# Prompt attention of a hybrid encoder step: weight blocks of which 16 queries are used, transposed from 32 rows

## The chip, the cores and the metric

The kernel runs on one core of one Trainium2 chip. The metric is the device time of one execution in microseconds; a number in a table is the median of the runs of a kernel, and one execution is also taken with the hardware profiler.

## The reference, cut to what matters

The reference computes one step of a one-layer streaming encoder: stick-breaking attention and a Mamba-2 state-space branch in parallel, a gated merge, and a causal convolutional FFN, for one new stream (16 meta tokens and 1024 frames) and for 8 running streams of 16 frames. The change lies in the attention of the new stream, 16 heads of 64 dimensions:

```python
def stick_breaking(q, k, v, q_pos, k_pos):
    z = jnp.einsum('bqhd,bshd->bhqs', q, k).astype(jnp.float32) * (SB_HEAD_DIM ** -0.5)
    reach = k_pos[None, :] < q_pos[:, None]
    log_beta = jax.nn.log_sigmoid(z)
    log_keep = jnp.where(reach, jax.nn.log_sigmoid(-z), 0.0)
    later = lax.cumsum(log_keep, axis=3, reverse=True) - log_keep
    w = jnp.where(reach, jnp.exp(log_beta + later), 0.0)
    return jnp.einsum('bhqs,bshd->bqhd', w.astype(v.dtype), v)
```

A query reaches only keys before it. So the weights `w` of a block of queries are zero from its own position on, and the transposed weights are needed only for the queries that reach a block of keys at all.

## The kernel before, in words

The program runs in phases: input norms, the state-space branch, the prompt attention (`phase_att`), the attention of the running streams (`phase_smp`), the merge, and the FFN. In `phase_att` the 16 heads follow each other (`head`, from L703), and projections of q, k, v and of the gates, which do not depend on the heads, are handed in between them (`paced`, L976) so that TensorE has other work while a head waits. The order of the instructions on each engine is not written out by hand: a scheduler of the framework works it out for the whole program from its own estimates of durations, and each engine then runs its list in that order.

A head works on its 1024 queries (the first two of 1026 are done elsewhere) in two groups g of four blocks i of 128 queries. For a block i:

- the scores of its queries against L = 144 + 128 i keys, `z` (L732, L735), on PE;
- a sigmoid on ACT (L695) into `beta`, the mask and 1 - beta on POOL (L741, L698), the running product over the keys from the end on DVE (L699), and the product that gives the weights, still in `beta` (L701).

The weights of a block lie with 128 queries on the partitions and keys along the row. The product with the values needs keys on the partitions, so each 128x128 piece is transposed by PE. `T_` (L133 to L135) does that: the piece is loaded as the stationary operand and the identity matrix streams through. For each block j of 128 keys up to 4g + 2, one PSUM tile `wT` takes the transposed pieces of the blocks i of the group side by side, 128 columns for each. There are two such buffers. The queries of block i sit at positions 16 + 128 i to 143 + 128 i, so of the queries of block i = j - 1 only the last 16 reach keys of block j. `b0` is therefore max(4g, j - 1), and `lo` skips 112 columns where the first piece is such a one; but the whole piece of 128 rows is transposed. ACT casts `wT` from `lo` on to a rounded high part `wTh` (L97), DVE takes the rest as `wTl` (L98), and two products on PE add both into `po`, tile `o` (L756, L759).

The remainder (from L760) holds the pieces (i, j) = (2, 4g + 3), (3, 4g + 3), (3, 4g + 4), where i counts within the group. They go into one `wT` tile at columns 0, 128 and 256, ACT copies columns 112 to 384 of it to `wf32` (L764), and plain float32 products of 144 and of 16 queries follow (L766). The first and the third of these pieces are used only in their last 16 queries. Then `att` is put together (L768, L769) and stored.

So in each group four transposes are of pieces of which only 16 queries are used: those at j = 4g + 1 and j = 4g + 2, and two in the remainder.

Of the kernel before, what the change touches and what calls it, by code (L numbers as in the profile page):

```python
# [13 lines left out]
F32 = mybir.dt.float32  # L14
# [63 lines left out]
class Kernel:  # L78
# [51 lines left out]
        l = self.tile(pool, [128, T], F32R, 'sl')  # L130
        return h, l

    def T_(self, out, in_, m=None):  # L133
        k = in_.shape[0]
        self.nc.tensor.transpose(out, in_, self.ident[:k, :k])  # L135


    def setup(self):
# [564 lines left out]
    def head(self, h, v):  # L703
        nc, ap, pa = self.nc, self.ap, self.pa
        marks = []
        rows = slice(64 * h, 64 * h + 64)
        KH, KL = (self.tile(ap, [128, TP], F32R, f'{n}{h % 2}', bufs=1) for n in ('KH', 'KL'))
        QS = self.tile(ap, [128, TP - T0], F32R, f'QS{h % 2}', bufs=1)
        VV = self.tile(ap, [128, 9, 128], F32R, f'VV{h % 2}', bufs=1)
        for r in (slice(0, 64), slice(64, 128)):  # L710
            nc.sync.dma_start(KH[r].bitcast(F32), self.s_kh[rows, 0:TP])
            nc.sync.dma_start(KL[r].bitcast(F32), self.s_kl[rows, 0:TP])
        nc.sync.dma_start(QS[0:64].bitcast(F32), self.s_qh[rows, 0:TP - T0])
        nc.sync.dma_start(QS[64:128].bitcast(F32), self.s_ql[rows, 0:TP - T0])
        nc.gpsimd.memset(VV[:, 8].bitcast(F32), 0.0)
        self.split(VV[:, 0:8, 0:64], VV[:, 0:8, 64:128], v[:, 0:8])
        self.split(VV[:16, 8, 0:64], VV[:16, 8, 64:128], v[:16, 8])
        for g in range(2):
            W = []
            for i in range(4 * g, 4 * g + 4):  # L720

                L = 144 + 128 * i
                np_ = -(-L // 512)
                step = -(-L // (2 * np_)) * 2
                B = self.tile(ap, [128, 256 + 128 * i], F32, f'beta{i}', bufs=1)
                pieces = []
                for c in range(0, L, step):
                    w = min(step, L - c)
                    wz = max(w, 256)
                    ps = self.tile(pa, [128, 512], F32, 'z', bufs=2)  # L730
                    q = QS[:, 2 + 128 * i:130 + 128 * i]
                    mm = nc.tensor.matmul(ps[:, :wz], q, KH[:, c:c + wz], start=True, stop=False)  # L732
                    if i % 2 == 0 and c == 0:
                        marks.append(mm)
                    nc.tensor.matmul(ps[:, :wz], q, KL[:, c:c + wz], start=False, stop=True)  # L735
                    pieces.append((ps[:, :w], c, w))
                nc.gpsimd.memset(B[:, L:128 * i + 256], 0.0)

                def mask():
                    d = B[:, L - 128:L]  # L740
                    nc.gpsimd.affine_select(out=d, in_=d, pattern=[[-1, 128]], base=0, channel_multiplier=1,  # L741
                                            compare_op=ALU.is_gt, fill=0.0)
                self.stick(pieces, B, 128, L, mask)
                W.append(B)
            po = self.tile(pa, [128, 512], F32, 'o', bufs=2)
            for j in range(4 * g + 3):

                b0 = max(4 * g, j - 1)
                lo = 128 * (b0 - 4 * g) + 112 * (b0 < j)
                pt = self.tile(pa, [128, 512], F32, 'wT', bufs=2)  # L750
                for i in range(b0, 4 * g + 4):
                    o = 128 * (i - 4 * g)
                    self.T_(pt[:, o:o + 128], W[i - 4 * g][:, 128 * j:128 * j + 128])
                wh, wl = (self.tile(ap, [128, 512], F32R, n) for n in ('wTh', 'wTl'))
                self.split(wh[:, lo:], wl[:, lo:], pt[:, lo:])
                mm = nc.tensor.matmul(po[:, lo:], VV[:, j, :], wh[:, lo:], start=(j == 0), stop=False)  # L756
                if j == 0:
                    self.pv_marks = [mm] if g == 0 else self.pv_marks + [mm]
                nc.tensor.matmul(po[:, lo:], VV[:, j, :], wl[:, lo:], start=False, stop=False)  # L759
            pt = self.tile(pa, [128, 512], F32, 'wT', bufs=2)  # L760
            for n, (i, j) in enumerate(((2, 4 * g + 3), (3, 4 * g + 3), (3, 4 * g + 4))):
                self.T_(pt[:, 128 * n:128 * n + 128], W[i][:, 128 * j:128 * j + 128])
            f = self.tile(ap, [128, 272], F32, 'wf32', bufs=1)
            nc.scalar.copy(f, pt[:, 112:384])  # L764
            for j, a0, n in ((4 * g + 3, 0, 144), (4 * g + 4, 256, 16)):
                nc.tensor.matmul(po[:, 512 - n:], VV[:, j, :].bitcast(F32), f[:, a0:a0 + n], start=False, stop=(n == 16))  # L766
            t = self.tile(ap, [64, 512], F32, 'att', bufs=1)
            nc.scalar.copy(t, po[64:128])  # L768
            nc.vector.tensor_tensor(out=t, in0=po[0:64], in1=t, op=ALU.add)  # L769
            nc.sync.dma_start(self.s_att[64 * h:64 * h + 64, 2 + 512 * g:514 + 512 * g], t)  # L770
        return marks
# [528 lines left out]
```

## Time and profile before

| | before |
|---|---|
| median of 3 runs | 2970.55 us (2970.44 to 2970.97) |
| the profiled execution | 2969.59 us |
| its span, first to last instruction | 2967.9 us |
| mean granted clock of TensorE | 0.994 |
| matmuls on PE | 17399 |

PE is TensorE's matmul side, PEld its weight loads, which run beside it; DVE, ACT and POOL are VectorE, ScalarE and GpSimd. In a row of a group of instructions stand line, engine, operation, tile written and tiles read, rows and columns of the loaded weights, shape and count, then the busy time in us, the mean of one in ns, and the idle time of the engine before them. The duration of a matmul is a latency and longer than the step to the next one; the step between two starts tells what one takes.

### The profile page before, as it was taken

What the parts mean: (1) busy time and instruction counts of PE and PEld (TensorE: products, weight loads), DVE (VectorE), ACT (ScalarE), POOL (GpSimd) and SP (SyncE); (2) the same over time, 40 slices, a digit from 0 to 9 for tenths busy, and PEclk for the clock granted to TensorE, in tenths of its full rate; (3) what the DMA queues carried; (4) which work ended last, traced back from release to release, by engine and by line L of the source; (5) the groups of instructions that cost most, each with busy time, mean ns of one, the idle gap of its engine ahead of it and who ended that gap; (6) DMA issues with size and microseconds to landing.
All of it is one profiled execution on the core that took longest, in us unless ns stands there. A gap on an engine that the chain in (4) does not pass through costs nothing.

```text
span 2967.9 us, 45503 instructions
## 1 busy us (share of the span) xinstructions
PE 2909.5 (98%) x17399; PEld 2764.3 (93%) x17399; DVE 1711.7 (58%) x2578; ACT 1259.3 (42%) x2611; POOL 626.7 (21%) x1009
## 2 busy tenths in 40 slices
PE   7999999999999999999999999999999999999998
PEld 6998988989889999999899899999999999999998
DVE  6457666676657777777634531446655454545447
ACT  5445454454444455544544310224534242424245
POOL 1024132231322233333333000003201010101013
PEclk9999999999999999999999999999999999999999
DMA  6435355354574555554344642545211111111113
GB/s 196 115 86 159 110 150 149 88 158 118 155 224 136 138 139 145 147 139 106 110 155 132 203 152 87 166 122 170 60 48 44 44 44 37 45 44 44 37 44 121
DMA packets 430826, 338.98 MB, mean 114 GB/s; under 512 B 27264, under 2 KB 406476, under 8 KB 430600
## 3 DMA queue, kind: packets, MB, share of 16 engines
q1 hardware_dynamic: 429103, 333.25, 39.1%
q8 instruction: 137, 2.24, 0.3%
q10 hardware_dynamic: 1504, 2.82, 0.3%
q14 instruction: 82, 0.66, 0.1%
HBM read 244.84 MB, written 91.67 MB: 113 GB/s over the span
## 4 chain that ended last, share of the span: by engine, by line
PE 84%; DMA 5%; DVE 3%; ACT 2%; issue 1%; POOL 1%; SPq 1%; DVEq 0%; ACTq 0%; POOLq 0%
PE mm L115 23%; PE mm L118 22%; PE mm L119 22%; PE wT L135 2%; DMA yt<-s_y 1%; PE yd L501 1%; PE z L732 1%; PE z L735 1%; PE st L484 1%; PE px L135 1%; PE o L759 1%; DMA zf<-s_z 1%; PE o L756 1%; PE yo L510 1%; DMA wf<-in_w_out 1%
## 5 line engine op out<-in xcount | busy, mean ns | idle before, releaser
L115 PE MATMUL mm<-sh,wh 128*128 128x384 f32 (+3 forms) x2520 | 869.2, 346 | 5.0 <-ACT sh L952 1.8
L118 PE MATMUL mm<-sl,wh 128*128 128x384 f32 (+3 forms) x2520 | 868.8, 345 | 3.4 <-DVE sl L98 2.6
L119 PE MATMUL mm<-sh,wl 128*128 128x384 f32 (+3 forms) x2520 | 864.3, 343 | 0.0
L118 PEld LDWEIGHTS mm<-sl,wh 128*128 128x128 f32 (+1 forms) x2520 | 474.9, 188 | 18.7 <-issue 10.3
L115 PEld LDWEIGHTS mm<-sh,wh 128*128 128x128 f32 (+1 forms) x2520 | 474.6, 188 | 16.3 <-issue 5.2
L119 PEld LDWEIGHTS mm<-sh,wl 128*128 128x128 f32 (+1 forms) x2520 | 474.8, 188 | 9.2 <-issue 7.5
L106 DVE TENSOR_TENSOR wl<-wf,wh 128x1024 fp32r<-128x1024 f32 (+2 forms) x205 | 253.3, 1236 | 305.8 <-ACT wh L105 304.7
L118 PE MATMUL mm<-pl,wh 128*128 128x386 f32 x1248 | 424.9, 340 | 0.0
L115 PE MATMUL mm<-ph,wh 128*128 128x386 f32 x1248 | 424.6, 340 | 0.0
L119 PE MATMUL mm<-ph,wl 128*128 128x386 f32 x1248 | 422.8, 339 | 1.2 <-DVE wl L106 1.1
L105 ACT CAST wh<-wf 128x1024 fp32r<-128x1024 f32 (+2 forms) x205 | 212.7, 1038 | 478.3 <-PE mm L118 455.9
L1167 DVE SCALAR_TENSOR_TENSOR acc<-fx,cwf,acc 128x384 f32<-128x384 f32 (+1 forms) x352 | 170.9, 516 | 155.4 <-ACT acc L1165 151.7
L119 PEld LDWEIGHTS mm<-ph,wl 128*128 128x128 f32 x1248 | 236.2, 189 | 2.3 <-DVE wl L106 1.8
L115 PEld LDWEIGHTS mm<-ph,wh 128*128 128x128 f32 x1248 | 236.3, 189 | 0.6
L118 PEld LDWEIGHTS mm<-pl,wh 128*128 128x128 f32 x1248 | 235.2, 188 | 1.7
L699 DVE TENSOR_TENSOR_SCAN keep<-keep 128x144 f32<-128x144 f32 (+7 forms) x128 | 180.1, 1409 | 52.0 <-POOL keep L698 51.3
L115 PE MATMUL mm<-ah,wh 128*128 128x384 f32 x528 | 179.7, 340 | 0.0
L119 PE MATMUL mm<-ah,wl 128*128 128x384 f32 x528 | 179.2, 339 | 0.0
L118 PE MATMUL mm<-al,wh 128*128 128x384 f32 x528 | 178.9, 339 | 0.0
L1094 POOL TENSOR_TENSOR sq<-sq,sq 128x386 f32<-128x386 f32 (+1 forms) x39 | 57.9, 1484 | 446.4 <-ACT sq L1093 438.5
L1192 DVE TENSOR_TENSOR h<-mm,h 128x384 f32<-128x384 f32 x144 | 79.7, 555 | 120.0 <-PE mm L119 119.5
L98 DVE TENSOR_TENSOR wTl<-wT,wTh 128x512 fp32r<-128x512 f32 (+3 forms) x176 | 102.9, 602 | 77.1 <-ACT wTh L97 76.4
(334 smaller groups left out, 4526.0 us busy)
## 6 DMA issues: line engine op xcount, KB each, us to landing
wf<-in_w_in SPq DMA_DIRECT2D x80, 512.0 KB
wf<-in_w_up SPq DMA_DIRECT2D x44, 512.0 KB
t<-s_ac SPq DMA_DIRECT2D x36, 512.0 KB
wf<-in_w_down SPq DMA_DIRECT2D x28, 512.0 KB
wf<-in_w_out SPq DMA_DIRECT2D x24, 512.0 KB
s_y<-x SPq DMA_DIRECT2D x16, 577.0 KB
yt<-s_y SPq DMA_DIRECT2D x16, 577.0 KB
KH<-s_kh SPq DMA_DIRECT2D x32, 260.0 KB
```

Of the source, the lines that this page charges most:

```text
L98: nc.vector.tensor_tensor(out=l, in0=x, in1=h.bitcast(F32), op=ALU.subtract)
L105: nc.scalar.copy(wh, wf)
L106: nc.vector.tensor_tensor(out=wl, in0=wf, in1=wh.bitcast(F32), op=ALU.subtract)
L115: i = nc.tensor.matmul(p, wh[:, k, :], mh[:, c:c + w], start=s, stop=False)
L118: nc.tensor.matmul(p, wh[:, k, :], ml[:, c:c + w], start=False, stop=False)
L119: nc.tensor.matmul(p, wl[:, k, :], mh[:, c:c + w], start=False, stop=e)
L135: self.nc.tensor.transpose(out, in_, self.ident[:k, :k])
L484: first = nc.tensor.matmul(pS, Bt, xe.rearrange("p h d -> p (h d)"), start=True, stop=True)
L699: nc.vector.tensor_tensor_scan(out=K[:, ::-1], data0=K[:, ::-1], data1=K[:, ::-1], initial=1.0, op0=ALU.mult, op1=ALU.min)
L1094: nc.gpsimd.tensor_tensor(out=acc[:, :w], in0=acc[:, :w], in1=sq, op=ALU.add)
L1167: nc.vector.scalar_tensor_tensor(out=op, in0=src(q), scalar=w(q), in1=op, op0=ALU.mult, op1=ALU.add)
L1192: self.nc.vector.tensor_tensor(out=h, in0=p, in1=h, op=ALU.add)
```

## The change

`T_` takes a first row `p0` in place of an argument that was not used, and uses the identity's block at that row and column. In the tiles j = 4g + 1 and 4g + 2 the piece with i < j is transposed from rows 96 to 127 alone, into the last 32 of its 128 columns. In the remainder the first and third piece are transposed the same way, and the three results lie closer: 32 columns at 0, 128 at 32, 32 at 160. The copy to `wf32` takes columns 16 to 192, 176 in place of 272, and the last product reads it at 160 in place of 256. What the products read is the same as before.

```diff
-    def T_(self, out, in_, m=None):
+    def T_(self, out, in_, p0=0):
         k = in_.shape[0]
-        self.nc.tensor.transpose(out, in_, self.ident[:k, :k])
+        self.nc.tensor.transpose(out, in_, self.ident[p0:p0 + k, p0:p0 + k])
...
                 for i in range(b0, 4 * g + 4):
                     o = 128 * (i - 4 * g)
-                    self.T_(pt[:, o:o + 128], W[i - 4 * g][:, 128 * j:128 * j + 128])
+                    r = 96 * (i < j)
+                    self.T_(pt[:, o + r:o + 128], W[i - 4 * g][r:, 128 * j:128 * j + 128], r)
...
             pt = self.tile(pa, [128, 512], F32, 'wT', bufs=2)
-            for n, (i, j) in enumerate(((2, 4 * g + 3), (3, 4 * g + 3), (3, 4 * g + 4))):
-                self.T_(pt[:, 128 * n:128 * n + 128], W[i][:, 128 * j:128 * j + 128])
-            f = self.tile(ap, [128, 272], F32, 'wf32', bufs=1)
-            nc.scalar.copy(f, pt[:, 112:384])
-            for j, a0, n in ((4 * g + 3, 0, 144), (4 * g + 4, 256, 16)):
+            for o, r, i, j in ((0, 96, 2, 4 * g + 3), (32, 0, 3, 4 * g + 3), (160, 96, 3, 4 * g + 4)):
+                self.T_(pt[:, o:o + 128 - r], W[i][r:, 128 * j:128 * j + 128], r)
+            f = self.tile(ap, [128, 176], F32, 'wf32', bufs=1)
+            nc.scalar.copy(f, pt[:, 16:192])
+            for j, a0, n in ((4 * g + 3, 0, 144), (4 * g + 4, 160, 16)):
```

## The prediction

> **What bounds the kernel now.** I read the head of the page first, then the busy time by stage, then the waits of TensorE inside the attention stage, and only then single instructions.
>
> ```profile
> span 2967.9 us, 45503 instructions
> PE 2909.5 (98%) x17399; PEld 2764.3 (93%) x17399; DVE 1711.7 (58%) x2578; ACT 1259.3 (42%) x2611; POOL 626.7 (21%) x1009
> ```
>
> ```profile
> 880.00:1476.00 596.00, 584.44 (x3624) 555.85 (x3622) 443.04 (x550) 293.99 (x671) 193.90 (x403) 1.00 0.50 134
> 1476.00:1660.00 184.00, 176.32 (x1037) 164.38 (x1038) 76.94 (x125) 81.19 (x160) 65.83 (x174) 0.95 0.46 141
> 1660.00:2968.00 1308.00, 1294.61 (x7375) 1281.36 (x7373) 645.24 (x1002) 458.78 (x821) 138.49 (x174) 1.00 0.27 83
> ```
>
> The numbers behind a stage are its length and then the busy time of PE, weight loads, DVE, ACT and POOL, and the granted clock. The first of these stages is the prompt attention (the heads run there, with projections between them). PE is busy for 584.44 of 596.00 us, so it idles 11.6 us in the whole stage, at full clock; the stages behind it are as full. What PE does more or less in a head therefore moves the end of the kernel, one for one, but for what fits into those 11.6 us. ACT (293.99) and DVE (443.04) have room.
>
> ```profile
> PE z L732 <- ACT beta L695: 4.2, 5, 1.6
> PE o L756 <- ACT wTh L97: 3.3, 4, 1.5
> PE o L759 <- DVE wTl L98: 1.3, 5, 0.4
> ```
>
> These are PE's waits in that stage (us in total, times, longest). None is ahead of a transpose of the weight blocks (L135, wT): these never start after an idle PE, so whatever they cost is paid by PE in full.
>
> **The change part by part.** A head has two groups of four query blocks. Full transposes now: group 0 makes 4, 4 and 3 in its tiles and 3 in the remainder, group 1 makes 4 in each of six tiles, 3 in the seventh and 3 in the remainder, which is 14 + 30 = 44 a head and 704 in 16 heads, as the trace has it:
>
> ```profile
> L135 PE MATMUL wT<-ident,beta 128*128 128x128 f32 x704 | 112.2, 273 | 0.0
> L135 PEld LDWEIGHTS wT<-ident,beta 128*128 128x128 f32 x704 | 88.9, 143 | 10.5
> L764 ACT COPY wf<-wT 128x272 f32<-128x272 f32 x32 | 12.6, 394 | 9.0 <-PE wT L135 8.6
> L766 PEld LDWEIGHTS o<-wf,VV 128*128 128x128 f32 x128 | 18.3, 189 | 0.1
> ```
>
> Of these, those with i < j become partial: one each in tiles j = 4g+1 and 4g+2, two of three in the remainder. That is 4 a group, 32 groups: 128 of the 704. A partial loads 32 rows by 128 columns as weights and streams 32 columns instead of 128. No instruction is added or taken away, no DMA and no wait; the queues of SP and POOL are untouched.
>
> *What a full transpose costs.* Its 273 ns is a latency; its price is the step to the next start.
>
> ```profile
> 1104.31 0.39 PE L756 MATMUL o<-wTh,VV 128*128 128x512 f32 x1
> 1104.54 0.38 PE L135 MATMUL wT<-ident,beta 128*128 128x128 f32 x2
> 1104.68 0.48 PE L759 MATMUL o<-wTl,VV 128*128 128x512 f32 x1
> 1105.00 0.82 PE L135 MATMUL wT<-ident,beta 128*128 128x128 f32 x6
> 1105.65 0.38 PE L135 MATMUL o<-ident,st 128*128 128x128 f32 x2
> ```
>
> (Start, duration, instruction, count of merged ones.) Six take 1105.00 to 1105.65, that is 0.11 us each. Nothing is lost on going in: the 512 columns of L756 before the first pair take 0.23 us to the next start, which is the same per column as the projections' 0.18 for 386 below.
>
> *What a partial will cost.* The heads have none now, but PE runs transposes with few rows elsewhere: the 16-row ones of the FFN's state (fs), the 24-row ones of the convolution's (sio), and one with 32 rows (fb). The first number of the shape, as in 16*128, is the rows of the weights.
>
> ```profile
> 2092.44 0.34 PE L115 MATMUL mm<-ph,wh 128*128 128x386 f32 x1
> 2092.62 0.34 PE L118 MATMUL mm<-pl,wh 128*128 128x386 f32 x1
> 2092.80 0.34 PE L119 MATMUL mm<-ph,wl 128*128 128x386 f32 x1
> 2093.07 0.29 PE L135 MATMUL tp<-ident,fs 16*128 16x16 f32 x2
> 2093.29 0.45 PE L115 MATMUL mm<-ph,wh 128*128 128x386 f32 x1
> 2093.57 0.34 PE L118 MATMUL mm<-pl,wh 128*128 128x386 f32 x1
> ```
>
> Ordinary matmuls step by 0.18 us. Into fs the step is 0.27, and the full matmul behind fs takes 0.28 to the next one. From 2092.80 to 2093.57 are 0.77 us; less two ordinary steps (0.36) the two small transposes cost 0.41. The second adds only 0.07 (0.29 merged, against 0.22 for one in the row of means below), so a lone one costs 0.34.
>
> ```profile
> 1442.98 0.36 PE L732 MATMUL z<-KH,QS 128*128 128x456 f32 x1
> 1443.19 0.28 PE L756 MATMUL o<-wTh,VV 128*128 128x272 f32 x1
> 1443.31 0.36 PE L735 MATMUL z<-KL,QS 128*128 128x456 f32 x1
> 1443.60 0.19 PE L135 MATMUL wT<-ident,fb 32*16 32x32 f32 x1
> 1443.73 0.44 PE L115 MATMUL mm<-sh,wh 128*128 128x386 f32 x1
> 1444.01 0.32 PE L732 MATMUL z<-KH,QS 128*128 128x348 f32 x1
> ```
>
> This one has the 32 rows and 32 columns of the change. From 1443.31 to 1444.01 are 0.70 us; less 0.21 for the 456 columns ahead (1442.98 to 1443.19) and 0.18 for the 386 behind, it costs 0.31.
>
> ```profile
> 556.44 0.34 PE L118 MATMUL mm<-sl,wh 128*128 128x386 f32 x1
> 556.62 0.33 PE L119 MATMUL mm<-sh,wl 128*128 128x386 f32 x1
> 556.88 0.24 PE L135 MATMUL ms<-ident,sio 24*128 24x24 f32 x1
> 557.04 0.49 PE L461 MATMUL ms<-bc,bc 128*128 128x128 f32 x2
> 557.46 0.24 PE L135 MATMUL ms<-ident,sio 24*128 24x24 f32 x1
> 557.63 0.33 PE L135 MATMUL ms<-ident,bc 128*128 128x128 f32 x1
> 557.72 0.42 PE L115 MATMUL mm<-sh,wh 128*128 128x386 f32 x1
> 558.07 0.42 PE L135 MATMUL ms<-ident,sio 24*128 24x24 f32 x4
> ```
>
> The same with 24 rows: 0.26 in instead of 0.18, 0.17 from it to a full transpose (557.46 to 557.63), whose own duration is then 0.33 in place of 0.27: its weights were not loaded ahead. So 0.08 going in, 0.17 for the partial and its way out, 0.06 of stall in the next: 0.31 again. That is the very neighbourhood of the change, since nearly every partial stands alone: first in its tile, behind a product and ahead of full ones, and in the remainder partial, full, partial.
>
> I take the middle of 0.31 and 0.34, rounded down to 0.32, as the 32-row case gave 0.31. Against 0.11 for a full transpose, each partial loses 0.21 us, and 128 of them 26.9 us. Bounds: if nothing is lost on changing over, a partial costs what four sio in a row cost, (0.42 - 0.24)/3 = 0.06, and the change gains 128 x 0.05 = 6.4 us; with 0.34 each it loses 128 x 0.23 = 29.4.
>
> What none of these rows shows is a partial at rows 96 to 127: all of them begin at row 0. I take the same price, since what they share is a narrow set of rows between full ones. The Trainium skill speaks to this in "TensorEngine Tiling (Array Packing)", Key Properties: a change of the tiling mode, and not only of the tile, drains TensorE. By that rule the position would not matter, and the sum stays at 26.9 us; without a drain it would be the gain of 6.4. The rows at row 0 agree with it (0.26 for 0.18).
>
> *The copy of the remainder* goes from 272 to 176 columns.
>
> ```profile
> L411 ACT COPY cin<-ms 128x144 f32<-128x144 f32 x4 | 1.1, 279 | 13.3 <-PE ms L135 13.3
> L135 PE MATMUL tp<-ident,fs 16*128 16x16 f32 x44 | 6.5, 220 | 0.0
> L135 PEld LDWEIGHTS tp<-ident,fs 16*128 16x128 f32 x44 | 4.3, 136 | 6.0 <-PE mm L119 4.2 <-issue 1.8
> ```
>
> Between 279 ns for 144 columns and 394 for 272, it will take some 0.31 us, 0.08 less, 2.7 us of ACT over 32 copies. The weight loads behind it (L766, above) idled 0.1 us in all, so PE does not wait for it: nothing gained. If PE came to wait for it, it would be 2.7 us at most. The products of the remainder keep their sizes (144 and 16).
>
> *Cover.* The 26.9 us can eat into the 11.6 us of idle. The 4.6 us of waits for wTh and wTl begin at the transposes and stay; of the 4.2 for beta a part may go. I take 2 off: 25. The profiled execution took 2969.59 us (its span and 1.7 us around it), 0.96 below the median of 2970.55; from there it is 2994.6, and on the median 2995.5.
>
> **The rivals.**
> *A, no stall at row 96, faster.* A narrow set of rows at the array's end passes without the pause, and a partial costs 0.06: 2970.55 - 6.4 = 2964.2. It decides once a partial costs less than the 0.11 of a full one. For it speaks only that no row shows that position; against it every small transpose above. 0.06.
> *B, the loads set the pace.* If a transpose steps at 0.11 because of its 128 weight columns, and nothing pauses, a partial costs the same 0.11 and nothing changes: 2970.6. For it: 136 ns for a load with 16 rows, against 143 for the full ones of the heads. Against it: the sio step of 0.06, with as many columns. The Trainium skill has this rule in "TensorE: Matmul & The Clock Gate", LDWEIGHTS: a load's time goes by columns, not rows. 0.05.
> *C, half of it covered.* The pause going in falls together with waits that PE has anyway, or the order of instructions, which is worked out anew, puts partials beside each other, where the second costs 0.07: half of 26.9, so 2984. Against: only 11.6 us of idle, none ahead of a transpose. 0.13.
> *D, knock-on.* Later transposes make the casts of ACT and the products wait longer, and PE's idle time doubles: 26.9 + 11.6, so 3009. 0.10.
>
> **How the numbers follow.** The forecast has the remaining 0.66, and 2990 to 3000 for itself (a partial at 0.31 with 6 us of cover, and at 0.34 with none). The range 2981 to 3006 takes in C and leaves out A, B and most of D, just under 2 in 10. Within 0.2%, 5.9 us, is what a measurement of this kernel can hardly tell from no change. Slower: the forecast, C and D, 0.89; within: B and a part of A, 0.06; faster: the rest of A, 0.05.
>
> **What would show it.** A group of 128 transposes wT with weights 32*128 and 32 columns, and 576 full ones in the heads; steps of about 0.26 us into a partial from 386 columns and of 0.17 from it to a full one; full ones behind it with 0.33. The attention stage should end about 25 us later and the stages behind keep their lengths. The copy wf near 0.31 us. It is wrong if the step from a partial is 0.06 to 0.08, or if it shows the pause but PE's idle time shrinks by as much.

## The result, and the profile after

| | before | changed |
|---|---|---|
| median | 2970.49 us (4 runs) | 2990.01 us (4 runs) |
| ratio | | 1.0065, interval 1.0053 to 1.0077 |
| second comparison, later | 2966.80 us (9 runs) | 2988.97 us (5 runs) |
| ratio there | | 1.0072, interval 1.0058 to 1.0085 |
| profiled execution (first) | 2969.59 us, span 2967.9 | 2989.64 us, span 2987.9 |

The change makes the kernel slower by 19.5 us (15.7 to 22.9 by the interval), and by 22.2 us in the second comparison (17.2 to 25.2). The forecast was 25.

The head of the page after, and then the same stage before and after, cut exactly from the first transpose of a weight block of the heads (tile wT from beta) to the first transpose of the next phase (wT from od). The stage is given from and to, then its length and the busy time of PE; first the row of the kernel before, then that of the changed one.

```profile
span 2987.9 us, 45520 instructions
PE 2932.3 (98%) x17399; PEld 2762.3 (92%) x17399; DVE 1713.6 (57%) x2578; ACT 1261.9 (42%) x2611; POOL 620.0 (21%) x1009
```
```profile
883.10:1503.90 620.80, 606.84 (x3741) 577.03 (x3740) 450.43 (x560) 302.30 (x685) 201.33 (x425) 0.99 0.50 135
```
```profile
879.50:1523.40 643.90, 633.28 (x3739) 579.52 (x3740) 452.83 (x562) 304.23 (x684) 193.50 (x425) 0.99 0.48 130
```

The stage grew by 23.1 us, and what follows it keeps its length (1464.0 us before, 1464.5 after). PE's busy time in the stage grew by 26.4, with the same number of instructions (the counts differ by two at the cut edges), and its idle time fell from 13.96 to 10.62. PE is busy longer with smaller instructions, because time in which a matmul is held up by its neighbour counts as busy here: below, the same kind of product lasts 0.48 us right behind a partial transpose and 0.37 us one place later.

The order of the instructions in the stage is not the same before and after. The scheduler worked it out anew, and on PE 1628 of the 17399 places hold another instruction. The same is so in most of the experiments below. Two of those with partials keep the changed kernel's order: the one with rows 0 to 31, and, but for the two transposes that it exchanges, the one with partials next to each other. The last kernel, with the padded transposes, keeps the order of the kernel before in this stage.

The groups of the changed kernel in the attention stage:

```profile
L135 PE MATMUL wT<-ident,beta 128*128 128x128 f32 x575 | 105.8, 282 | 0.0
L135 PE MATMUL wT<-ident,beta 32*128 32x32 f32 x127 | 30.9, 243 | 0.0
L135 PEld LDWEIGHTS wT<-ident,beta 32*128 32x128 f32 x127 | 16.9, 133 | 25.6 <-issue 6.7 <-PE z L735 3.4 <-PE o L760 3.3
```

The partial transposes are there (these rows are of the stretch from 880 to 1500 us, which begins just behind the first of each kind; all 576 and 128 are in the trace). Two readings: the mean of the full ones rose from 273 to 282 ns, since those behind a partial last longer; and the weight loads of the partials, 133 ns with 32 rows against 143 for full ones, are now preceded by 25.6 us of idle on the side of the loads, 0.20 us for each of the 127, while the same tile's loads were idle for 10.5 us in 704 before. These loads are not brought forward beside the running matmul: in the remainder shown next the load of the first partial begins at 1008.36, together with its matmul, but that of the product ahead of it at 1007.91, 0.17 us before its own. One remainder of the changed kernel, instruction by instruction (start, duration):

```profile
1008.09 0.34 PE L760 MATMUL o<-wTl,VV 128*128 128x400 f32 x1
1008.36 0.24 PE L135 MATMUL wT<-ident,beta 32*128 32x32 f32 x1
```
```profile
1008.53 0.33 PE L135 MATMUL wT<-ident,beta 128*128 128x128 f32 x1
```
```profile
1008.53 0.50 PE L135 MATMUL wT<-ident,beta 128*128 128x128 f32 x2
1008.96 0.48 PE L732 MATMUL z<-KH,QS 128*128 128x456 f32 x1
1009.28 0.37 PE L735 MATMUL z<-KL,QS 128*128 128x456 f32 x1
```

0.27 from a product of 400 columns into the partial, 0.17 from it to the full transpose, which lasts 0.33, then the second partial, which begins at about 1008.79 (the pair ends at 1009.03, a partial lasts 0.24). From 1008.09 to 1009.28 are 1.19 us. Less 0.18 for the 400 columns and 0.21 for the first z, the three transposes cost 0.80; three full ones cost 0.33. That is 0.235 more for each of the two partials.

This is one remainder. Added up over the whole stage, group of transposes by group, and set against what groups of full ones with the same neighbours take in the kernel before, a partial costs about 0.21 us more than a full transpose in the tiles and about 0.24 in the remainder, some 28 us for all 128 (27 to 29, by how the steps are compared).

### The profile page after: what moved, and what is told of

Its sections match the earlier page's. It is cut to its first block, busy times and chain, and to the rows that moved or that the text cites. A ratio compares the mean times of both kernels' runs of the same rounds, so it can differ in the third digit from the quotient of the medians.

```text
span 2987.9 us, 45520 instructions
## 1 busy us (share of the span) xinstructions
PE 2932.3 (98%) x17399; PEld 2762.3 (92%) x17399; DVE 1713.6 (57%) x2578; ACT 1261.9 (42%) x2611; POOL 620.0 (21%) x1009
## 4 chain that ended last, share of the span: by engine, by line
PE 86%; DMA 4%; DVE 3%; ACT 1%; issue 1%; SPq 0%; POOL 0%; DVEq 0%; ACTq 0%; POOLq 0%
PE mm L115 23%; PE mm L118 23%; PE mm L119 23%; PE wT L135 4%; PE z L732 1%; PE z L735 1%; PE o L760 1%; PE o L757 1%; PE yd L501 1%; PE st L484 1%; DMA yt<-s_y 1%; DMA zf<-s_z 1%; PE px L135 1%; PE yo L510 1%; PE tp L135 1%
```

## The experiments

The first question was whether the loss goes with the number of partials and their price, or with something that the change does besides: a new order of instructions, the remainder's packing, the position in the array. Each comparison has runs of the kernel before of its own.

**Half the partials: the tiles alone**

```diff
 # before, with the new T_; the remainder as before
+                    r = 96 * (i < j)
+                    self.T_(pt[:, o + r:o + 128], W[i - 4 * g][r:, 128 * j:128 * j + 128], r)
```

> Only the 64 partial transposes of the tiles j = 4g + 1 and 4g + 2 are made from 32 rows; the remainder is as before the change. Theory (every partial pays for two change-overs of TensorE, 0.32 us in place of 0.11): 64 x 0.21 = 13.4 us gross, some 2 covered, so half of the change's loss, 2979 to 2983. Rival (the loss comes from the new order of the instructions or from the remainder's alternating partial, full, partial): under a quarter of it, 2970 to 2975, or all of it, 2988 and more.

Measured: 2974.13 us against 2968.09, ratio 1.0019 (1.0011 to 1.0028): 6.0 us (3.3 to 8.3 by the interval), less than the 11 to 15 expected. The time lies in the 2970 to 2975 that were named for the rival, a new order of instructions or the remainder's alternation as the cause. But the steps in this trace show the full price: the 64 partials and their neighbours take some 13 us more than full transposes. So the partials are not cheap here; PE made up for half of their price or more elsewhere in the stage, as the rows behind the next run show. That the order is not the cause of the loss, this run alone does not show; the one with partials next to each other does.

**The other half: the remainder alone**

```diff
 # the change, but in the tiles
-                    r = 96 * (i < j)
+                    r = 0
```

> Only the 64 partial transposes of the remainder (partial, full, partial, and the shorter copy); the tiles j = 4g + 1 and 4g + 2 use all 128 rows. Theory (each partial costs the same and what a stage does not show is taken from idle time): the two halves add up to the change, so about 13 us over the kernel before, after 6 for the tiles alone. Rival (the tiles-only run was low because partials ahead of three full transposes are cheaper): the steps into and out of a partial differ between the two runs; then 8 us or less here would leave 5 us of the change unexplained.

Measured: 2976.53 us against 2967.13, ratio 1.0029 (1.0017 to 1.0040): 9.4 us (5.0 to 11.9), where 13 were expected. The stage of the two, tiles alone first:

```profile
880.10:1505.30 625.20, 616.82 (x3740) 576.40 (x3741) 452.51 (x562) 303.99 (x684) 198.40 (x425) 0.99 0.49 134
```
```profile
879.20:1508.00 628.80, 618.56 (x3741) 578.10 (x3741) 451.96 (x562) 301.55 (x685) 196.82 (x425) 0.99 0.49 133
```

PE's busy time rose by 10.0 and 11.7 us over 606.84 where 64 x 0.21 would be 13.4, and the idle time went down to 8.4 and 10.2. So each half costs, neither costs its full price, and the idle time takes up more of a half than was thought: 5.6 us with the tiles alone. Which waits gave way there can be read from the waits of PE in its stage:

```profile
PE z L732 <- ACT beta L695: 2.6, 3, 1.0
PE o L760 <- DVE wTl L98: 1.7, 6, 0.4
```

Before it was 4.2 us for beta and 1.3 for wTl. The 3.3 us for wTh are gone altogether, and so is one wait of 1.3 us for Ksh at L889, behind the heads. The prediction had expected the waits for wTh to stay. Whether they went because the products come later or because of the new order, these runs do not separate. The two halves by the runs make 15.4 us and the change 19.5 to 22.2; the intervals are as wide as that gap, so a true difference is not shown.

**Partials next to each other**

```diff
-((0, 96, 2, 4 * g + 3), (32, 0, 3, 4 * g + 3), (160, 96, 3, 4 * g + 4))
+((32, 0, 3, 4 * g + 3), (0, 96, 2, 4 * g + 3), (160, 96, 3, 4 * g + 4))
```

> As the change, but in the remainder the full transpose goes first and the two partials follow each other; nothing else in the order of the instructions is moved. Theory: one change-over in and one out less in each of 32 remainders, the second partial of a pair costs 0.07 to 0.09 in place of 0.32, so 32 x 0.24 = 7.6 us less than the change, 2981 to 2984. Rival (a narrow transpose is slow by itself, wherever it stands): no difference, 2989 to 2991.

Measured: 2980.85 us against 2968.09, ratio 1.0044 (1.0032 to 1.0057): 12.8 us (9.5 to 16.9) in place of the change's 19.5 to 22.2, with as many partials and, but for the exchange, the same order on every engine. The same remainder as above:

```profile
1009.91 0.35 PE L760 MATMUL o<-wTl,VV 128*128 128x400 f32 x1
1010.10 0.27 PE L135 MATMUL wT<-ident,beta 128*128 128x128 f32 x1
```
```profile
1010.30 0.30 PE L135 MATMUL wT<-ident,beta 32*128 32x32 f32 x2
1010.53 0.48 PE L732 MATMUL z<-KH,QS 128*128 128x456 f32 x1
1010.85 0.37 PE L735 MATMUL z<-KL,QS 128*128 128x456 f32 x1
```

From the product to the second z 0.94 us in place of 1.19: the three cost 0.55 in place of 0.80. 32 x 0.25 = 8.0 us by the steps, 6.7 to 9.4 by the medians, which come from different comparisons. A partial right behind a partial does not pay: it follows after about 0.08 us. The price is one of changing over, and not of the small transpose. This tells the theory from its rival most plainly, and a new order cannot have done it.

**Other rows, and more rows**

```diff
 # rows 0 to 31 (the weights of other queries)
-self.T_(pt[:, o + r:o + 128], W[i - 4 * g][r:, 128 * j:128 * j + 128], r)
+self.T_(pt[:, o + r:o + 128], W[i - 4 * g][:128 - r, 128 * j:128 * j + 128])
 # and likewise in the remainder
...
 # in the other run, the last 64 rows
-                    r = 96 * (i < j)
+                    r = 64 * (i < j)
```

> As the change, with the same order of instructions, but the partials take rows 0 to 31 in place of 96 to 127 (so the weights of other queries are used in those 16 columns). Theory (what counts is that few rows are used, not which): as the change, 2988 to 2992, with the same steps into and out of a partial. Rival (the position at the end of the array makes it slower or quicker): more than 3 us off the change.

> As the change, but the partials take the last 64 rows and stream 64 columns (the copy of the remainder then has 208 columns). Theory (any set of rows other than all of them pays the change-over): the pause stays and 32 more columns at about 0.8 ns each (0.03 us) come on top, so 128 x 0.03 = 3.4 us over the change, 2991 to 2996. Rival (only sets of 32 rows pay): steps of about 0.08 and no pause, 2965 to 2968.

Measured: rows 0 to 31 2987.18 us against 2968.09, ratio 1.0065 (1.0051 to 1.0078), as the change. With 64 rows 2989.14, ratio 1.0073 (1.0060 to 1.0085). The stage with rows 0 to 31, and then the same tile in both, a partial and two full transposes between a product and a z, first with rows 0 to 31 and then with 64 rows:

```profile
884.40:1526.10 641.70, 631.31 (x3740) 578.42 (x3741) 453.13 (x562) 304.41 (x684) 193.17 (x425) 0.99 0.47 130
```
```profile
1011.96 0.35 PE L757 MATMUL o<-wTh,VV 128*128 128x400 f32 x1
1012.24 0.61 PE L135 MATMUL wT<-ident,beta 32*128 32x32 f32 x3
1012.60 0.43 PE L732 MATMUL z<-KH,QS 128*128 128x392 f32 x1
```
```profile
1009.49 0.35 PE L757 MATMUL o<-wTh,VV 128*128 128x400 f32 x1
1009.76 0.27 PE L135 MATMUL wT<-ident,beta 64*128 64x64 f32 x1
```
```profile
1009.76 0.64 PE L135 MATMUL wT<-ident,beta 64*128 64x64 f32 x3
1010.16 0.43 PE L732 MATMUL z<-KH,QS 128*128 128x392 f32 x1
```

(A row with x3 counts the two full transposes with the partial, whose shape it gives.) Going in takes 0.28 and 0.27 from a product of 400 columns, as in the change. So neither the position nor the number 32 matters for the pause; being fewer rows than the neighbours does. The 3.4 us more that 64 columns should cost are within what the times leave open, but they are there in the steps: from a partial to the next instruction it is 0.20 us in the mean of all 128 with 64 rows and 0.17 with 32.

**All rows, few columns**

```diff
-        self.nc.tensor.transpose(out, in_, self.ident[p0:p0 + k, p0:p0 + k])
+        if c0:
+            self.nc.tensor.matmul(out, in_, self.ident[:, c0:], start=True, stop=True)
+        else:
+            self.nc.tensor.transpose(out, in_, self.ident[:k, :k])
 # c0 is 96 for the 128 pieces, which are handed in with all 128 rows of W
```

> The 128 pieces are turned from all 128 rows, as plain float32 products with the last 32 columns of the identity, which the profile shows as two instructions each, in place of transposes from 32 rows; the packing is that of the change. Theory (it is the few rows that pay): no pause of 0.08 ahead of them and no full transposes of 0.33 behind them; two short products of some 0.07 to 0.09 each in place of 0.11, so 128 x 0.05 = 6 us over the kernel before, 2971 to 2977 against 2968. Rival (any narrow result pays): 2987 and more.

Measured: 2976.52 us against 2967.13, ratio 1.0032 (1.0021 to 1.0044): 9.4 us. Its steps:

```profile
1005.66 0.28 PE L760 MATMUL o<-wTh,VV 128*128 128x272 f32 x1
1005.79 0.30 PE L136 MATMUL wT<-ident,beta 128*128 128x32 f32 x2
1005.93 0.31 PE L138 MATMUL wT<-ident,beta 128*128 128x128 f32 x1
1006.07 0.31 PE L136 MATMUL wT<-ident,beta 128*128 128x32 f32 x2
```

0.13 for the 272 columns ahead, as without any pause, and 0.14 for two products and 0.14 for the full transpose behind them: 0.17 for a piece where a full transpose takes 0.11. It loses too, for the two products that float32 needs, but by 0.06 a piece and not 0.21, and with as few columns as the change streams. As far as this run tells, the few rows pay, not the few columns. The order of instructions differs from the change's here, and these are plain products. A transpose of this kernel streams as many columns as it has rows, so for transposes themselves no run separates the two; the next run gives them all of both.

**The other way round: few rows made full where the kernel already had them**

```diff
 # before; fs is one tile of [128, 2, 128], set to zero once, of which 16 rows are loaded
-            self.T_(pf[:, 16 * e:16 * e + 16], fs[:, e])
+            self.T_(pf[:, 16 * e:16 * e + 128], fs[:, e])
```

> The kernel before, without the change; in the FFN the 16-row transposes of the state (fs, 22 pairs) are turned from 128 rows, of which 112 are zeros. Theory (a pair costs 0.41 us for its change-overs and would cost 0.22 as two full ones): 22 x 0.19 = 4.2 us less than before, 2963 to 2965 against 2968. Rival (the pause is hidden or comes from something else near these transposes): no difference.

Measured: 2962.55 us against 2967.13, ratio 0.9985 (0.9976 to 0.9994): 4.6 us (1.8 to 7.1) faster than the kernel before, the fastest version here. The price is read here in a part of the program that the change does not touch, with the order of the attention as before.

```profile
2085.19 0.34 PE L119 MATMUL mm<-ph,wl 128*128 128x386 f32 x1
2085.36 0.38 PE L135 MATMUL tp<-ident,fs 128*128 128x128 f32 x2
2085.50 0.43 PE L115 MATMUL mm<-ph,wh 128*128 128x386 f32 x1
2085.76 0.34 PE L118 MATMUL mm<-pl,wh 128*128 128x386 f32 x1
```

From the matmul ahead to the second behind are 0.57 us, where the 16-row pair took 0.77. Eight times the rows and columns, and 0.20 us less: the prediction's price, read backwards. Over all 22 pairs of the two traces these stretches add up to 4.4 us less.

**The change once more**

> The changed kernel itself once more, with more runs beside the kernel before. The first comparison gave 15.7 to 22.9 us, and the attention stages of two profiled executions each (with the same order of instructions) differ by 22 to 24. If the halves add up (6 for the tiles, 9 for the remainder) the change should come out at 15 to 18; if the price of 0.21 us for each of 128 with some 3 to 4 us of idle time taken up holds, at 21 to 24.

Measured: the 22.2 us given above. Its stage, after that of the padded kernel, whose attention has the same instructions in the same order as the kernel before:

```profile
878.70:1498.00 619.30, 606.15 (x3740) 576.10 (x3741) 451.11 (x562) 302.36 (x684) 201.56 (x425) 0.99 0.50 135
```
```profile
881.10:1522.50 641.40, 631.24 (x3741) 578.10 (x3742) 453.10 (x562) 304.53 (x684) 192.47 (x425) 0.99 0.48 130
```

22.1 us for the stage, 25.1 for PE's busy time, and 13.15 of idle down to 10.16: the first pair of executions over again.

## Why the prediction was right, point by point

- *The price of a partial.* Right. Forecast were 0.08 going in, 0.17 out and 0.06 in the next; the changed kernel has 0.27 for 0.18 or 0.19, 0.17, and 0.33 in place of 0.27. 128 x 0.21 = 26.9 us was the sum; by the steps of all partials it is some 28, and PE's busy time in the stage rose by 26.4 and 25.1. That prices of 16 and 24 rows at row 0 hold for 32 rows at row 96 was an assumption, taken for want of a row, with a chance against it; the run with rows 0 to 31 and that with 64 rows bear it out. The Trainium skill says in "TensorEngine Tiling (Array Packing)", Key Properties, that changing the tiling mode, and not just the tile, drains TensorE. The pause of 0.08 to 0.09 us with either set of rows, and its absence between two partials (0.08 in all), agree with that; no run here goes from one tile to another of the same mode, so that half of the rule is not shown.
- *The cover.* This term was mis-sized: 2 us forecast, 3.3 and 3.0 by idle time, and some 5 or 6 when the growth of the stage is set against the 28 us of the steps; the rest came out of steps between other instructions, and no run here separates what the new order did in them. Of the named waits that for beta gave way, from 4.2 to 2.2 us, and those for wTh and wTl stayed (4.6 before, 4.4 after), as forecast for the change, though not with the tiles alone:

```profile
PE o L757 <- ACT wTh L97: 3.5, 5, 1.2
PE z L732 <- ACT beta L695: 2.2, 4, 1.0
PE o L760 <- DVE wTl L98: 0.9, 4, 0.2
```

- *The sum.* 25 forecast, 23.1 and 22.1 in the stage, 19.5 and 22.2 in the medians. The price was a little too low and the cover too low by 3 or 4 us, so a small part of the agreement is luck. The time lies at the lower edge of the 2990 to 3000 that the forecast had for itself, and that edge was named for a partial at 0.31 with 6 us of cover, which is near what the traces show. The profiled execution before also lost time ahead of the stage, which starts at 883.1 us there and at 879.5 after, with the same instructions in the same order up to it. It lost it in two short stretches at a lower granted clock: the mean was 0.91 over the first 60 us and 0.95 from 850 to 883 us, where the changed kernel's execution has 1.00 in both. One of them, before and then after, in the same series of projections:

```profile
49.45 0.52 PE L119 MATMUL mm<-sh,wl 128*128 128x384 f32 x1
49.77 0.52 PE L115 MATMUL mm<-sh,wh 128*128 128x384 f32 x1
50.09 0.52 PE L118 MATMUL mm<-sl,wh 128*128 128x384 f32 x1
```
```profile
47.80 0.34 PE L119 MATMUL mm<-sh,wl 128*128 128x384 f32 x1
47.97 0.34 PE L115 MATMUL mm<-sh,wh 128*128 128x384 f32 x1
48.15 0.34 PE L118 MATMUL mm<-sl,wh 128*128 128x384 f32 x1
```

  Steps of 0.32 in place of 0.18, for a few us. Where the stage begins differs by up to 5.7 us between the executions of all kernels here (878.7 to 884.4 us), though PE has the same instructions in the same order up to there. In the first pair of profiles this hid 3.6 us of the difference.
- *The copy.* 307 ns for 176 columns, as worked out (0.31 us); nobody waited for it.

```profile
L765 ACT COPY wf<-wT x32: 306/307/323, 896.6 to 1493.1; 128x176 f32<-128x176 f32 x32
```

- *The rivals.* A (no pause at row 96) falls by the steps. B (the loads set the pace) falls by the pair of partials, where the second took about 0.08 with a load of 128 columns. C was right in direction: some 5 or 6 us of 28 were covered in the change, and half or more with the tiles alone; the scheduler put no two partials beside each other. D did not come: idle time fell.

What stays open is why the tiles alone came out at 6.0 us when the steps into and out of their partials look like all the others. 5.6 us came out of idle time in the one execution that was profiled, most of it the waits for wTh and beta; why PE never waited for wTh there, and 3.5 us in the change, and what the order of instructions had to do with it, no run here shows.

## What to carry to other kernels

Before cutting a matrix instruction down to the rows it needs, look in the trace for the step ahead of and behind any instruction that already has few rows: if the neighbours have all rows, a lone narrow transpose here cost about 0.32 us with its two change-overs, and a full one 0.11. Put narrow ones next to each other (the second costs 0.08), or fill them up with zeros to all rows, which here gained 4.6 us where the kernel had narrow ones of old. By these figures it takes some eight to ten narrow ones in a row to be as quick as as many full ones; that is an estimate, and no run here has such a row of them. On an engine that is busy 98% of the time most of such a price goes into the end (19.5 to 22.2 us of some 28), but of the price of the 64 in the tiles alone the stage hid half or more. Count it in the steps, since the busy share does not show it as idle.

## What the runs showed of the hardware

Two things that the prediction had not said: that 64 rows pay as 32 do (0.27 from a product of 400 columns in both, and 0.20 in place of 0.17 on the way out); and that the idle time of the weight loads grows so plainly with it (25.6 us in front of 127 loads, against 10.5 in front of 704), which makes that column of the groups the quickest place to see such change-overs.
